# The third weave string of a two-layer decoder trunk: preparation steps placed one by one, gate columns at the end

## The chip, the cores and the metric

One core of one Trainium2 chip runs the whole program. The metric is device time in microseconds (us): the median of three runs of the kernel before is 1687.29 us, with the lowest at 1686.63 and the highest at 1689.68. The engines are named as in the profile: PE (matrix products and transposes), DVE (vector), ACT (activation), POOL (general purpose), SP (issues loads).

## The reference, cut to what matters

A trunk of two layers over 512 tokens of width 1024. In each layer five attention branches read one projection of the input; each branch's output is projected by its own matrix and scaled by a sigmoid gate of the input; the sum goes through one output matrix, and a mixture of experts follows.

```python
o_moba = merge_heads(moba_attention(heads(q, N_MOBA_HEADS), heads(k, N_MOBA_HEADS), heads(v, N_MOBA_HEADS),
                                    alibi_slopes(N_MOBA_HEADS)))
o_mla = mla_attention(c_q, c_kv, k_rope_in, g_cq, g_ckv, w_uq, w_ukv)
...
for i, o in enumerate((o_sb, o_moba, o_mla, o_nsa, o_mem)):
    gate = jax.nn.sigmoid(x @ w_gate[i] + b_gate[i])
    merged = merged + gate * (o @ w_br[i])
return merged @ w_out
```

The latent attention (`mla_attention`) first normalizes two low-rank inputs, then forms keys and values from one and queries from the other, and turns 32 columns of key and query by position (rope).

## The kernel before

All products are done three times, on values split in two parts (`hi` on ACT, L93, and the residual `lo` on DVE, L108), so nearly every product is followed by one ACT and one DVE instruction that read it from PSUM, or has such a pair ahead of it for its weights. PSUM has eight tiles of 128x512: three with the tag `f`, two `s`, two `pt`, one `pv` (L1682). Instructions run in the order of their engine's queue; the tile framework orders them by the program, and a tile with a tag waits until the readers of the tile that had its place are done.

`mixer` (L911) runs five stages in each layer. In each of them `weave` (L867) takes steps from up to three generators by a string: one letter, one step. The third stage, at about 197 to 359 us in layer 0 and 1039 to 1200 us in layer 1, has

- `a`, 20 steps, `moba_att` (L456): four heads with five steps each. For each of four query blocks `score_block` (L240) multiplies scores into an `s` tile, adds a strip and takes the minimum on DVE (L254), takes the exponent on ACT (L259) and scales on DVE (L260, L262); `to_pt` transposes into `pt`, and ACT and DVE copy that to `pth` and `ptl`. The fifth step multiplies by the values into `pv` and adds two halves (L280, L281).
- `g`, 16 steps, `gates` (L777): eight columns of the gate of the branch before (stick-breaking attention), two steps each. The first splits the weights (`wh`, from a load in `rw`; `bh`), runs 24 products into an `f` tile (L166) and takes the tanh on ACT (`gt`, L788). The second runs six products of the branch's output into another `f` tile (L116), which DVE multiplies into `gt` (L797) and POOL adds to `mg` (L798).
- `q`, 13 steps, `mla_qkv` (L469), which prepares the next stage's latent attention. In order: the input `c_kv` (with 24 products into `f`); the two parts of `c_q`; the rotary key; normalizing and weights `uw`; two steps for two pairs of heads' keys (`qk`); two steps for the values, two tiles each (step 7 writes the first two, step 8 the other two, each read by an ACT and a DVE cast into a tile with the tag `v`, of which there are six); a step that scales `c_q` (`mt` to `cp`, L534, L101, L113); and four query heads, of which each runs six products into an `f` tile and then reads it with L99 on ACT and L113, L591, L592 on DVE.

The values of MoBA (four `v` tiles) are read by the `pv` products until its last head is done, so two of the latent attention's four `v` tiles can be written only then. After the stage come preparations of the fourth branch (L625 and on) in the same `f` tiles.

Of the kernel before, what the change touches and what calls it, by code (L numbers as in the profile page):

```python
# [70 lines left out]
class Trunk:  # L71
# [1568 lines left out]
    qs = "pp"  # L1640
    wq = "ssss"
    busy_e = 3
    orders = ('aaaqaaaaqaaaaaaaaaaaaqqa', 'gggqqgaaaaggaaaaaaggaaaaqqggggggaqqqqagagaaa', 'qaagaaggagqqaggaaaqaggaqaaaaqggaqqaaaaggqggqqggqq', 'ggqgaaaaaaaaaaagqgaaaggqagggggggqqqqgaaaaga', 'ggaaaaaaaaaggggggggaaaaaaaaaaaaaaaagaaaaaaaaaagggagg')
    x1 = 0

    class _Pool:
# [66 lines left out]
```

## Time and profile before

| | us |
|---|---|
| median of three runs | 1687.29 |
| profiled execution | 1692.76 |
| its span | 1690.9 |
| PE busy in it | 1597.3 (94%) |
| DVE busy | 1248.6 (74%) |
| ACT busy | 866.4 (51%) |
| POOL busy | 258.4 (15%) |

The mean granted clock of the span is 0.977. A view of waits lists, for an engine, which line waited for which instruction; a group of lines gives the mean duration of one instruction; a table of stretches gives the busy time of each engine in a piece of the span, and the clock that TensorE was granted there.

### The profile page before, as it was taken

The numbers are of one execution on the slowest core, as the hardware profiler recorded it, in microseconds if no ns is written. First come the engines' busy times: TensorE is split into PE (matmuls) and PEld (weight loads), VectorE is DVE, ScalarE is ACT, GpSimd is POOL, SyncE is SP. The second block draws the span as 40 slices with busy tenths as digits, with TensorE's granted clock in tenths as the row PEclk, the third lists the DMA queues.
The fourth block names the chain that finished last, engine by engine and source line by source line (L and its number), as shares of the span: only waits on it lengthen the run. The fifth ranks groups of instructions, "written<-read, shape, count | busy, mean of one in ns | idle before, by whom it ended". The sixth has DMA issues, their size and how long they took to land. (4 is left out here: it accounts for less than half of the span.)

```text
span 1690.9 us, 22740 instructions
## 1 busy us (share of the span) xinstructions
PE 1597.3 (94%) x7936; PEld 1265.6 (75%) x7936; DVE 1248.6 (74%) x2557; ACT 866.4 (51%) x1655; POOL 258.4 (15%) x212
## 2 busy tenths in 40 slices
PE   8999999999999998999699999999999999999995
PEld 6877877778777786666587778777777787766673
DVE  6777558864885678998788766488657946899987
ACT  5644446343563425788436444463434733367871
POOL 0000011101112111233300000111111111113332
PEclk9999999989999998999799999999999999999998
DMA  8232222434337757998542322223332186489964
GB/s 254 66 84 79 73 70 63 113 99 126 98 91 252 248 188 254 384 376 304 194 137 57 97 72 75 74 57 95 83 93 58 49 290 220 165 308 374 380 220 156
DMA packets 254565, 273.62 MB, mean 162 GB/s; under 512 B 38667, under 2 KB 191361, under 8 KB 254433
## 3 DMA queue, kind: packets, MB, share of 16 engines
q1 hardware_dynamic: 241032, 223.98, 41.4%
q0 software_dynamic: 13312, 47.98, 8.2%
q8 instruction: 67, 1.10, 0.3%
q14 instruction: 66, 0.53, 0.1%
q10 hardware_dynamic: 88, 0.03, 0.0%
HBM read 239.18 MB, written 32.77 MB: 161 GB/s over the span
## 5 line engine op out<-in xcount | busy, mean ns | idle before, releaser
L166 PE MATMUL f<-xh,wh 128*128 128x512 f32 (+2 forms) x1920 | 630.8, 397 | 2.5 <-ACT xh L97 1.5
L166 PEld LDWEIGHTS f<-xh,wh 128*128 128x128 f32 (+1 forms) x1920 | 355.6, 188 | 77.4 <-ACT xh L97 1.7
L166 PE MATMUL f<-xl,wh 128*128 128x512 f32 (+2 forms) x960 | 381.1, 397 | 0.0
L112 DVE TENSOR_TENSOR wh<-rw,wh 128x1024 fp32r<-128x1024 f32 (+1 forms) x174 | 228.4, 1317 | 51.0 <-ACT wh L97 49.9
L798 POOL TENSOR_TENSOR mg<-mg,gt 128x512 f32<-128x512 f32 x64 | 96.8, 1512 | 984.9 <-DVE gt L797 984.9
L166 PEld LDWEIGHTS f<-xl,wh 128*128 128x128 f32 (+1 forms) x960 | 180.7, 188 | 36.6 <-DVE xl L112 0.2
L97 ACT CAST wh<-rw 128x1024 fp32r<-128x1024 f32 (+3 forms) x178 | 178.7, 1012 | 53.9 <-PE f L192 15.5
L788 ACT ACTIVATE gt<-f,bgh 128x512 f32<-128x512 f32 x80 | 55.0, 688 | 210.9 <-PE f L166 210.8
L116 PE MATMUL f<-wh,xh 128*112 128x512 f32 (+1 forms) x564 | 157.1, 404 | 5.9 <-DVE wh L112 5.8
L116 PE MATMUL f<-oh,bh 128*128 128x512 f32 x480 | 131.2, 400 | 0.2
L116 PEld LDWEIGHTS f<-wh,xh 128*112 128x112 f32 (+1 forms) x564 | 98.7, 180 | 35.9 <-DVE wh L112 7.4
L97 ACT CAST pth<-pt 128x128 fp32r<-128x128 f32 (+1 forms) x192 | 77.4, 418 | 87.3 <-PE pt L124 81.5
L797 DVE SCALAR_TENSOR_TENSOR gt<-gt,f 128x512 f32<-128x512 f32 x64 | 43.8, 684 | 105.7 <-PE f L116 101.2
L116 PE MATMUL f<-eh,xh 128*112 128x512 f32 (+1 forms) x396 | 111.0, 400 | 1.6 <-DVE eh L112 1.6
L112 DVE TENSOR_TENSOR ptl<-pt,pth 128x128 fp32r<-128x128 f32 (+1 forms) x192 | 88.8, 473 | 24.7 <-ACT pth L97 23.1
L97 ACT CAST wh<-rp 128x1024 fp32r<-128x1024 f32 x84 | 87.3, 1053 | 33.6 <-PE pt L116 14.3
L112 DVE TENSOR_TENSOR wh<-rp,wh 128x1024 fp32r<-128x1024 f32 x74 | 97.9, 1338 | 8.5 <-ACT wh L97 7.9
L116 PE MATMUL s<-qk,qk 128*128 128x256 f32 (+7 forms) x416 | 98.5, 334 | 6.0 <-DVE st L254 2.7
L116 PEld LDWEIGHTS f<-oh,bh 128*128 128x128 f32 x480 | 89.0, 190 | 19.8 <-issue 1.0
L124 PE MATMUL pt<-ident,ne 128*128 128x128 f32 x472 | 83.7, 279 | 8.6 <-DVE ne L433 3.8
L116 PEld LDWEIGHTS s<-qk,qk 128*128 128x128 f32 (+1 forms) x416 | 66.9, 192 | 27.1 <-DVE st L254 9.3
L124 PEld LDWEIGHTS pt<-ident,ne 128*128 128x128 f32 x472 | 54.7, 141 | 42.4 <-issue 17.1
(355 smaller groups left out, 2723.7 us busy)
## 6 DMA issues: line engine op xcount, KB each, us to landing
rp<-in_w_up_dram SPq DMA_DIRECT2D x96, 512.0 KB, 14.0
rw<-in_w_gate_dram SPq DMA_DIRECT2D x80, 512.0 KB, 3.9
rp<-in_w_down_dram SPq DMA_DIRECT2D x48, 512.0 KB, 14.9
rw<-in_w_in_dram SPq DMA_DIRECT2D x38, 512.0 KB, 3.9
rw<-in_w_out_dram SPq DMA_DIRECT2D x32, 512.0 KB, 6.8
yd<-xl POOLq DMA_DIRECT2D x28, 448.0 KB, 6.9
xl<-xd POOLq DMA_DIRECT2D x24, 448.0 KB, 7.6
rb<-in_w_br_dram SPq DMA_DIRECT2D x80, 128.0 KB, 3.4
```

Source lines behind the costliest of these rows:

```text
L97: return nc.scalar.copy(out, in_)
L112: return e.tensor_tensor(out, in_, hi.bitcast(F32), ALU.subtract)
L116: self.nc.tensor.matmul(out, lhsT, rhs, start=start, stop=stop)
L124: return self.nc.tensor.transpose(out, in_, self.ident[:k, :k])
L166: self.nc.tensor.matmul(o[:M, n], a[:, k, :M], b[:, k, n], start=c + k + m == 0, stop=k == KT - 1 and m == 2, skip_group_check=cut > 1)
L788: nc.scalar.activation(t, gp, AF.Tanh, bias=self.bgh[:, b * 8 + f : b * 8 + f + 1], scale=0.5)
L797: nc.vector.scalar_tensor_tensor(t, t, 1.0, bp, ALU.add, ALU.mult)
L798: i = nc.gpsimd.tensor_tensor(m, m, t, ALU.add)
```

## The change

One string of `orders` (L1643), the one of the third stage, is another; the letters are the same in number (20 `a`, 16 `g`, 13 `q`), so the instructions are the same and only their order in the queues of this stage differs, in both layers.

```diff
-    orders = ('aaaqaaaaqaaaaaaaaaaaaqqa', 'gggqqgaaaaggaaaaaaggaaaaqqggggggaqqqqagagaaa', 'qaagaaggagqqaggaaaqaggaqaaaaqggaqqaaaaggqggqqggqq', 'ggqgaaaaaaaaaaagqgaaaggqagggggggqqqqgaaaaga', 'ggaaaaaaaaaggggggggaaaaaaaaaaaaaaaagaaaaaaaaaagggagg')
+    orders = ('aaaqaaaaqaaaaaaaaaaaaqqa', 'gggqqgaaaaggaaaaaaggaaaaqqggggggaqqqqagagaaa', 'qaaqgaagqaqgaqgaaqaggaqaqaagqagaqqgaaqgagagqagggg', 'ggqgaaaaaaaaaaagqgaaaggqagggggggqqqqgaaaaga', 'ggaaaaaaaaaggggggggaaaaaaaaaaaaaaaagaaaaaaaaaagggagg')
```

Before, the string ends with gate columns between the last query heads; after, with two gate columns in a row (`gggg`), and the last `q` stands five letters from the end. The names below carry a number: `f_469` is one tile.

The first place is PE near the end of MoBA, where the value steps of the latent attention (`f` written from `uw`) stand. Before, the last three of four value tiles and what follows:

```order
L116 MATMUL f_499_2677<-uw_445_2450,cp_442_2442 128x256 x3
L116 MATMUL f_501_2684<-uw_445_2450,cp_442_2442 128x256 x3
L116 MATMUL f_503_2691<-uw_445_2450,cp_442_2442 128x256 x3
L116 MATMUL s_507_2705<-qk_290_1583,qk_202_1174 128x256
L116 MATMUL s_507_2705<-qk_291_1584,qk_202_1174 128x256
L116 MATMUL s_511_2719<-qk_290_1583,qk_202_1174 128x384
L116 MATMUL s_511_2719<-qk_291_1584,qk_202_1174 128x384
L116 MATMUL f_505_2698<-uw_445_2450,cp_442_2442 128x256 x3
L166 MATMUL f_525_2772<-xh_1_102,wh_524_2769 128x512
L166 MATMUL f_525_2772<-xl_2_103,wh_524_2769 128x512
```

After, the last two value tiles, `f_469` and `f_471`:

```order
L116 MATMUL pv_456_2485<-pth_420_2338,v_324_1853 128x128
L116 MATMUL pv_456_2485<-ptl_421_2339,v_324_1853 128x128
L116 MATMUL f_469_2527<-uw_413_2298,cp_410_2290 128x256 x3
L116 MATMUL f_471_2534<-uw_413_2298,cp_410_2290 128x256 x3
L116 MATMUL s_477_2555<-qk_288_1577,qk_201_1171 128x384
L116 MATMUL s_477_2555<-qk_289_1578,qk_201_1171 128x384
```

and, after the 24 products of `f_485`, PE goes on so:

```order
L116 MATMUL s_491_2622<-qk_288_1577,qk_201_1171 128x512
L116 MATMUL s_491_2622<-qk_289_1578,qk_201_1171 128x512
L116 MATMUL f_495_2638<-oh_382_2132,bh_482_2572 128x512 x3
L116 MATMUL f_495_2638<-oh_383_2135,bh_482_2572 128x512 x3
L116 MATMUL s_518_2748<-qk_290_1583,qk_202_1174 128x128
L116 MATMUL s_518_2748<-qk_291_1584,qk_202_1174 128x128
L116 MATMUL s_522_2761<-qk_290_1583,qk_202_1174 128x256
L116 MATMUL s_522_2761<-qk_291_1584,qk_202_1174 128x256
L116 MATMUL f_499_2666<-cp_488_2613,uw_498_2659 128x512 x2
L124 MATMUL pt_494_2631<-ident_84,ne_492_2625 128x128 x4
L116 MATMUL f_499_2666<-cp_488_2613,uw_498_2659 128x512
L116 MATMUL f_499_2666<-cp_489_2617,uw_498_2659 128x512 x3
```

Before, the last value tiles are followed by one gate column (`f_525`) and the last attention blocks. Now they stand before a gate column (`f_485` with `f_495`), two query heads (`f_499`, `f_505`), another gate column (`f_514`) and a third query head (`f_527`), since the fourth head of MoBA (`s_518` and on, up to `pv_554`) is still to come.

The second place is ACT where the last two value tiles are read. Before, the readers (`v_504`, `v_506`) stand behind the last transposes of MoBA:

```order
L97 CAST pth_493_2662<-pt_514_2728 128x3x128
L97 CAST pth_493_2662<-pt_518_2743 128x4x128
L97 CAST v_504_2695<-f_503_2691 128x4x64
L97 CAST v_506_2702<-f_505_2698 128x4x64
L280 COPY ot_520_2759<-pv_519_2750 64x512
L788 ACTIVATE gt_526_2797<-f_525_2772,bgh_60_472 128x512
L97 CAST wh_575_3028<-rw_574_3026 128x1024
```

After, `f_469` and `f_471` are read (`v_470`, `v_472`) behind the readers of `f_499`, `f_505`, `f_514` and `f_527`:

```order
L99 ACTIVATE qk_500_2673<-ot_502_2677 32x512
L99 ACTIVATE qk_506_2698<-f_505_2691 64x512
L259 ACTIVATE ne_544_2864,st_545_2865<-ne_544_2864,st_545_2865 128x512
L99 ACTIVATE qk_506_2698<-ot_508_2702 32x512
L788 ACTIVATE gt_515_2744<-f_514_2719,bgh_60_472 128x512
L97 CAST pth_516_2746<-pt_536_2818 128x3x128
L97 CAST pth_516_2746<-pt_546_2870 128x4x128
L97 CAST wh_566_2976<-rw_565_2974 128x1024
L99 ACTIVATE qk_528_2789<-f_527_2782 64x512
L97 CAST v_470_2531<-f_469_2527 128x4x64
L97 CAST v_472_2538<-f_471_2534 128x4x64
```

The readers of the last two value tiles moved behind two query heads and a gate column that were written later than these tiles.

The third place is ACT at the end of the stage, where `f_580` (L625, the fourth branch's first product, copied by L627 into `peT`) needs an `f` tile. Before, two query heads stand ahead of the column `gt_577`:

```order
L97 CAST bh_588_3119<-rb_587_3117 128x256
L97 CAST wh_590_3124<-rw_589_3122 128x1024
L99 ACTIVATE qk_560_2979<-f_559_2972 64x512
L99 ACTIVATE qk_566_3004<-f_565_2997 64x512
L99 ACTIVATE qk_560_2979<-ot_562_2983 32x512
L788 ACTIVATE gt_577_3056<-f_576_3031,bgh_60_472 128x512
L97 CAST wh_649_3380<-rw_648_3378 128x1024
L627 COPY peT_581_3074<-f_580_3071 128x32
```

After:

```order
L788 ACTIVATE gt_561_2958<-f_560_2933,bgh_60_472 128x512
L97 CAST wh_583_3079<-rw_582_3076 128x1024
L97 CAST bh_573_3023<-rb_572_3021 128x256
L788 ACTIVATE gt_568_3004<-f_567_2979,bgh_60_472 128x512
L97 CAST wh_590_3124<-rw_589_3122 128x1024
L97 CAST oh_570_3015<-oo_359_2022 128x512
L97 CAST oh_571_3018<-oo_462_2511 128x512
L97 CAST bh_588_3119<-rb_587_3117 128x256
L788 ACTIVATE gt_577_3056<-f_576_3031,bgh_60_472 128x512
```

The query heads (`qk_560`, `qk_566` before) are gone from here; gate columns alone stand ahead of `gt_577`.

## Rows read from the trace of the kernel before

**Rows 1.** Page, part 1: engine, busy us, share of the span, instructions.

```profile
PE 1597.3 (94%) x7936; PEld 1265.6 (75%) x7936; DVE 1248.6 (74%) x2557; ACT 866.4 (51%) x1655; POOL 258.4 (15%) x212
```

**Rows 2.** PE waits, 175 to 335 us: total us, times, longest us.

```profile
PE s L116 <- DVE st L254: 1.1, 2, 0.8
PE f L625 <- ACT gt L788: 1.1, 1, 1.1
PE pt L124 <- DVE ne L262: 0.8, 1, 0.8
PE f L166 <- DVE ot L592: 0.5, 1, 0.5
PE pt L124 <- DVE ne L433: 0.4, 2, 0.2
```

**Rows 3.** Stretches: length, busy us of each engine, then granted clock, DMA share, GB/s.

```profile
310.00:315.00 5.00, 3.40 (x15) 2.14 (x14) 4.80 (x8) 2.17 (x4) 0.00 (x0) 1.00 0.36 105
315.00:320.00 5.00, 4.98 (x15) 3.96 (x16) 4.50 (x5) 1.10 (x4) 2.21 (x2) 0.66 0.33 90
```

**Rows 4.** Timeline around the tail: start, us, engine, instruction, idle before and its releaser.

```profile
314.20 0.29 PE L625 MATMUL f<-ident,kt 16*128 16x16 f32 x2 [1.09 <-ACT gt L788]
...
315.02 0.54 PE L166 MATMUL f<-xh,wh 128*128 128x512 f32 x1 [0.53 <-DVE ot L592]
```

**Rows 5.** Timeline, PE inside a gate column.

```profile
211.07 0.40 PE L166 MATMUL f<-xh,wh 128*128 128x512 f32 x1
211.31 0.39 PE L166 MATMUL f<-xl,wh 128*128 128x512 f32 x1
```

**Rows 6.** Timeline, value tiles of the latent attention.

```profile
273.27 1.46 PE L116 MATMUL f<-uw,cp 128*128 128x256 f32 x9
...
282.90 0.72 ACT L97 CAST v<-f 128x256 fp32r<-128x256 f32 x2 [1.31 <-PE pv L116]
...
283.30 0.77 DVE L112 TENSOR_TENSOR v<-f,v 128x256 fp32r<-128x256 f32 x2 [0.99 <-ACT v L97]
```

**Rows 7.** Groups by line and shape, ACT, 184 to 340 us: busy, mean ns, idle before.

```profile
L97 ACT CAST wh<-rw 128x1024 fp32r<-128x1024 f32 x16 | 16.7, 1042 | 8.1 <-PE f L166 6.2 <-DMA rw<-in_w_gate_dram 1.6 <-PE f L192 0.3
L788 ACT ACTIVATE gt<-f,bgh 128x512 f32<-128x512 f32 x11 | 7.6, 689 | 15.4 <-PE f L166 15.3
...
L259 ACT ACTIVATION_READ_ACCUMULATOR ne<-ne,st 128x1 f32 x16 | 3.0, 188 | 0.0
...
L259 ACT ACTIVATE ne<-ne,st 128x512 f32<-128x512 f32 x4 | 2.9, 721 | 1.2 <-DVE st L254 1.2
...
L101 ACT ACTIVATE cp<-mt,pcol 128x512 fp32r<-128x512 f32 x3 | 2.1, 720 | 0.8 <-DVE mt L534 0.8
```

**Rows 8.** Groups by line and shape, DVE, 184 to 340 us.

```profile
L112 DVE TENSOR_TENSOR wh<-rw,wh 128x1024 fp32r<-128x1024 f32 x16 | 20.6, 1288 | 3.4 <-ACT wh L97 3.2
L797 DVE SCALAR_TENSOR_TENSOR gt<-gt,f 128x512 f32<-128x512 f32 x10 | 6.8, 684 | 5.3 <-PE f L116 5.2
L112 DVE TENSOR_TENSOR bh<-rb,bh 128x256 fp32r<-128x256 f32 x11 | 6.8, 617 | 0.0
...
L112 DVE TENSOR_TENSOR ptl<-pt,pth 128x512 fp32r<-128x512 f32 x5 | 3.4, 689 | 2.3 <-ACT pth L97 2.3
...
L112 DVE TENSOR_TENSOR v<-f,v 128x256 fp32r<-128x256 f32 x8 | 3.2, 418 | 4.1 <-ACT v L97 4.1
L260 DVE RECIPROCAL st<-st 128x1 f32<-128x1 f32 x20 | 3.1, 153 | 0.3 <-ACT ne L259 0.2
...
L592 DVE TENSOR_TENSOR ot<-f,rope 32x512 f32<-32x512 f32 x4 | 2.8, 696 | 0.1
...
L254 DVE CUSTOM_DVE_ANT_0 ne<-s,strip 128x384 f32<-128x384 f32 x4 | 2.2, 547 | 0.7 <-PE s L116 0.7
```

**Rows 9.** Stretches around another long PE wait of this kernel.

```profile
864.00:868.00 4.00, 1.84 (x11) 1.28 (x10) 4.00 (x10) 0.00 (x0) 1.46 (x1) 1.00 0.00 0
868.00:872.00 4.00, 3.94 (x22) 3.68 (x21) 4.00 (x7) 1.53 (x3) 0.00 (x0) 0.57 0.78 253
```

## Prediction

> **What bounds the kernel now.** I read the page's busy times first: PE works 94% of the span and DVE 74% [rows 1], so the time moves only where PE stops or its clock falls. The table of waits for PE in the stage lists everything that PE waited for there in layer 0, 3.9 us [rows 2]; the names and sizes in layer 1 are the same within 0.1. Of it, 1.6 stand at the end of the stage: the fourth branch's first transpose (L625) waits 1.09 for a tanh that frees an `f` tile, and the next column 0.53 more [rows 4]. Behind these two waits TensorE's granted clock is 0.66 for 5 us, a mix of its levels 1.2 and 2.4 GHz, after 1.0 (2.4 GHz) [rows 3]: 0.34 x 5 = 1.7 us lost. So the stage loses 3.9 + 1.7 = 5.6 us a layer. That is all that a better order of the stage can give back, 11 us in two layers.
>
> **What the change removes.** The tail. The query heads, with four wide DVE passes each behind one product group, no longer stand between the last gate columns; the gate column needs one such pass. The L625 product then finds a tile that was read a column earlier. Gone: 1.09 + 0.53 + 1.7 = 3.3 us a layer. I see nothing that takes its place there, since a column gives PE 30 products, 30 x 0.24 = 7.2 us [rows 5], while DVE has about 3.4 us to do for it.
>
> **What it adds: two `f` tiles held.** The two last value tiles (`f_469`, `f_471`) are written before the fourth MoBA head, but their readers need `v` places that only the last `pv` product frees. Before, such a hold is visible too: the products at 273.27, their readers at 282.90 behind an idle ACT that waited 1.31 for `pv` [rows 6]. It cost nothing, because PE had one 24-product column and attention to do, and no second `f` tile was asked for. After, six groups (`f_485`, `f_495`, `f_499`, `f_505`, `f_514`, `f_527`) pass through the one `f` tile that is left, each behind the last reader of the one before. I follow PE's list and the readers' list side by side with the durations of before. PE's pace for a 512-column product is 0.24 [rows 5]; smaller ones I take by their columns. An instruction that follows another on ACT or DVE costs about 0.07 less than its own duration (two `v` residuals take 0.77 together, one takes 0.418) [rows 6, 8]. A hand-over between engines I take as 0.15 to 0.27.
>
> - `f_499` after `f_495`: counted from the end of `f_485`, ACT runs `gt` 0.69, `wh` 1.04, two `cp` 1.44, the exponent 0.72 and its read-out 0.19 [rows 7]; DVE follows with the reciprocal 0.15, which waits for that exponent, and the gate product 0.68 [rows 8]. With hand-overs 0.4 and less 0.4 of overlap, 4.9. PE has four transposes, two scores, six products of `f_495` and four small scores to do, 0.4 + 0.5 + 1.4 + 0.4, and a wait of 0.15 for the same `gt`: 2.85. **Wait 2.1.**
> - `f_505` after `f_499`: DVE reads `f_499` last in L592, sixteenth behind the gate product: `wh` 1.29, `bh` 0.62, five 512-wide ones at 0.69 (the rows are `ptl` and L592), and nine small ones from 0.08 to 0.55 (first and last rows: reciprocal, 384-wide reduction), together 3.2 [rows 8]: 8.5, less 16 x 0.07 = 7.4. PE has 4.2 of work: six products, four transposes, four scores, one `pv` group of eight and three transposes. **Wait 3.2**, part of it ahead of `pv` and the transposes.
> - `f_514` after `f_505`: two small ones, a sum, a reduction, and the four query passes in DVE's list come to 4.8, less 0.5 of overlap plus a hand-over, 4.45; PE has 1.4 + 0.65. **Wait 2.4.**
> - `f_527` waits 0.4 for the tanh of `f_514`, its `pv` group 0.1, and `f_532` 0.95 for the first value residual, which stands behind a `wh` of 1.29 on DVE. **1.45.** With 0.3 for `f_495` and a score behind it, this stretch comes to 0.3 + 2.1 + 3.2 + 2.4 + 1.45 = **9.4**.
>
> The Trainium skill, page "Perfetto Trace Analysis", section "Identifying Performance Opportunities", says that the same gap repeating on the engine that should be saturated can mean that there is no SBUF or PSUM left for the next tile. The trace of before has no repeating gap in this stage; by the rule the trace after would have one, at `f`.
>
> **What it adds further ahead.** An earlier place has the same shape: a gate column (`f_453`) wants the tile of a key pair (`f_426`), whose last reader stands in DVE's list behind a `wh` residual, a reciprocal, two casts and two residuals. Counted from the end of the column before, tanh 0.69, `wh` 1.04 and 1.29, and 0.7 + 1.4 + 0.7 of passes no shorter than [rows 8] shows, less the overlap: 5.8, against 3.6 of PE work: 2.2. Smaller waits of transposes and `pv` for scaled scores I sum to 1.3, the stage's start to 0.7 (0.4 before), and the 0.8 at the first head's transposes stays [rows 2]: its list of instructions is the same. Together 5.0.
>
> **The sum.** After: 9.4 + 5.0 = 14.4 us a layer; before: 5.6. Per layer +8.8, in two layers +17.6. The clock: another long wait of this kernel (PE busy 1.84 of 4 us) is followed by 4 us at 0.57, which costs 1.7 [rows 9]. The stretch has three waits of that size, and while the clock is low the waits behind it shorten, since they run against ACT and DVE; I take half of one fall a layer, 1.7 in all. Total +19.3. Against the profiled execution's own 1692.76 this is 1712.1; the median of the runs lies 5.5 below that execution, 1687.29 + 19.3 = 1706.6.
>
> Bounds: below, the waits that chains of few instructions give, without the small ones: 1.9 + 2.5 + 1.85 + 0.5, with 1.0 for `f_453`, 0.4 for the start and 0.8 that stays, 9.0, so +3.4 a layer or +7: 1694. Above, 16 us a layer and three us of low clock, 2 x 13.4 = +27: 1714. Loads cost nothing: the order of the weights on SP's queue hardly changes, and they are issued long ahead; a wait for one could shrink or grow by about 1 us. POOL's sums (L798) move with their gate columns; a DVE instruction beside one can take longer, which is why `bh` has a mean of 0.62 here, and I keep that mean.
>
> **The rivals.**
>
> - *The held tiles are covered.* If the readers of `f_499`, `f_505` and `f_514` came as early as before, when they cost no wait, only the tail would count: -3.3 a layer, 1687.3 - 6.6 = 1681. It decides from the point where each of the three reader lists is shorter than PE's work beside it (2.85, 4.2 and 2.05). For it: DVE has a quarter of its time free. Against it: the lists are 4.9, 7.4 and 4.45 long by rows of before, and each would have to lose 2 us or more. By the Trainium skill, page "Perfetto Trace Analysis", section "Identifying Performance Opportunities", interleaving regimes in which another engine is the most contended may improve the time; this change interleaves DVE-heavy query heads with PE-heavy gate columns, and by that rule this case would be the right one.
> - *They cancel.* The `f` waits come to 3 us a layer in place of 9.4, and the early ones to about what was there: 1687. For it: hand-made chains add up every step; against it, the three long waits would all have to be a third of their size.
> - *The clock falls at each long wait.* Four falls a layer (with `f_453`) of 1.7, half of them hidden: 3.4 in place of 0.85, +5.1: 1712. For it: it stands behind waits of 1.6 and 2.2 [rows 3, 9]. Against it: not every wait of that size in the trace need be followed by one.
> - *The tail stays.* If L625 still waits (`gt_577` comes late all the same): +6.6, 1713. Against it: nothing that reads a query head is left there.
>
> **How the numbers follow.** My forecast has 0.70, the clock 0.10, the tail 0.04, the cancelling case 0.08 and the covered tiles 0.08. A measurement of this kernel can tell about 0.2%, 3.4 us, from no change. The forecast is slower over all of its own range, as are the clock and the tail: slower 0.84; within 0.2%: 0.08; faster 0.08. The range goes from 1692, a little below the lower bound, to 1716, above the clock case; it leaves out the two cases at or below 1687 and a little above.
>
> **What would show it.** In the waits of PE after: `f` L116 behind DVE L797 and L592 with about 2 to 3 us each, `f` L166 behind L592 with 2 or more, in both layers; no L625 wait; ACT's `v` casts behind the last `pv`. Wrong would be: no wait of PE at `f` above 1 us in the stage (then the lists are shorter than their durations say), or an L625 wait that stays. If the waits are there and the time is still lower, something behind the stage took up the slack.

## The result

The kernel after takes 1706.57 us (median of 6 runs, 1702.2 to 1716.26), the kernel before 1686.96 (6 runs, 1685.16 to 1689.68). The ratio is 1.0110, 95% interval 1.0093 to 1.0126: slower by 1.1%. The forecast was 1706.6 in a range of 1692 to 1716. The mechanism is the one forecast; two terms of the sum were not, and their errors nearly cancelled, as shown below. The profiled execution of after took 1704.7 us with a span of 1702.9, 12 us over the profiled execution of before; the medians are 19.6 apart.

The waits of PE in the stage of layer 0, in the kernel after (the view of [rows 2]: who waited for whom, total us, times, longest):

```profile
PE f L116 <- DVE ot L592: 1.9, 1, 1.9
PE f L166 <- DVE ot L592: 1.7, 1, 1.7
PE f L116 <- DVE gt L797: 1.7, 1, 1.7
PE f L166 <- DVE qk L112: 1.6, 1, 1.6
PE pt L124 <- DVE ne L262: 1.4, 4, 0.7
PE pv L116 <- DVE ptl L112: 0.6, 2, 0.4
PE f L116 <- DVE v L112: 0.5, 1, 0.5
PE pt L124 <- DVE ne L433: 0.5, 2, 0.3
```

Four long waits at `f` tiles are new (three of them behind the two held tiles, the one behind L112 ahead of them), and the L625 row is gone. Layer 1 has the same rows within 0.1 us. In the table of stretches, from the first L480 to the first L625 of a layer (length, busy us of PE, PEld, DVE, ACT, POOL, then granted clock, DMA share, GB/s), the kernel before in layer 0 reads

```profile
199.49:314.20 114.71, 111.16 (x537) 86.97 (x536) 82.32 (x185) 62.42 (x137) 14.89 (x9) 1.00 0.26 75
```

and the kernel after, in both layers,

```profile
199.81:324.77 124.96, 114.95 (x543) 89.93 (x541) 86.80 (x191) 61.56 (x136) 15.96 (x9) 0.99 0.23 64
1043.75:1170.18 126.43, 116.73 (x542) 91.59 (x540) 86.85 (x191) 61.60 (x136) 15.97 (x9) 0.96 0.23 63
```

The stage is 10.3 and 11.7 us longer. PE's idle time in it (length less PE busy) goes from 3.6 to 10.0 and 9.7. The rest, 3.8 and 5.6 us, is PE busy for longer: six score products of the next stage now stand ahead of L625 (543 products against 537), 1.3 us, and the clock is low for a while. In layer 0 of after it falls once, behind the waits at 277 and 282 us (4-us stretches of after):

```profile
278.00:282.00 4.00, 2.31 (x11) 1.38 (x9) 3.86 (x8) 2.04 (x4) 0.00 (x0) 1.00 0.00 0
282.00:286.00 4.00, 3.72 (x10) 2.94 (x11) 3.85 (x13) 0.62 (x1) 0.00 (x0) 0.58 0.00 0
```

The 0.58 costs 0.42 x 4 = 1.7 us. In layer 1, where the two waits end at 1121.4 and 1126.4, the low stretch begins behind the first of them and is longer, 5.1 us by the same sum:

```profile
1120.00:1124.00 4.00, 2.60 (x10) 2.05 (x11) 3.77 (x9) 1.48 (x5) 0.00 (x0) 0.79 0.05 8
1124.00:1128.00 4.00, 2.37 (x8) 1.81 (x8) 3.69 (x8) 1.47 (x4) 0.00 (x0) 0.50 0.02 4
1128.00:1132.00 4.00, 4.00 (x11) 3.13 (x10) 2.29 (x8) 0.11 (x1) 0.00 (x0) 0.50 0.33 89
1132.00:1136.00 4.00, 3.93 (x20) 3.00 (x20) 0.00 (x0) 0.85 (x2) 0.00 (x0) 0.93 0.14 43
```

This sum is an upper bound: PE stands idle in a part of the low time (busy 2.37 of 4 us at 0.50), and the stage of layer 1 is 1.5 us longer than that of layer 0, not 3.4.

The tail is as forecast. Where [rows 3] showed 0.66, the stretch behind L625 is at full clock, without a wait:

```profile
325.00:330.00 5.00, 5.00 (x23) 4.04 (x23) 3.27 (x3) 0.59 (x3) 2.29 (x2) 1.00 0.45 112
```

The one `f` tile that passes from hand to hand can be followed in the timeline of after (start, us, engine, instruction, idle before and its releaser):

```profile
265.38 0.69 ACT L788 ACTIVATE gt<-f,bgh 128x512 f32<-128x512 f32 x1 [2.62 <-PE f L166]
...
269.06 0.68 DVE L797 SCALAR_TENSOR_TENSOR gt<-gt,f 128x512 f32<-128x512 f32 x1
...
269.89 0.70 PE L116 MATMUL f<-cp,uw 128*128 128x512 f32 x2 [1.66 <-DVE gt L797]
...
276.62 0.70 DVE L592 TENSOR_TENSOR ot<-f,rope 32x512 f32<-32x512 f32 x1
...
277.46 1.63 PE L116 MATMUL f<-cp,uw 128*128 128x512 f32 x6 [1.95 <-DVE ot L592]
...
281.44 0.69 DVE L592 TENSOR_TENSOR ot<-f,rope 32x512 f32<-32x512 f32 x1
...
282.28 0.47 PE L166 MATMUL f<-xh,wh 128*128 128x512 f32 x1 [1.74 <-DVE ot L592]
...
293.41 0.75 DVE L112 TENSOR_TENSOR v<-f,v 128x256 fp32r<-128x256 f32 x2
...
293.88 1.66 PE L116 MATMUL f<-oh,bh 128*128 128x512 f32 x6 [0.51 <-DVE v L112]
```

Three times the last reader ends on DVE (start and duration added: 269.74, 277.32, 282.13), and 0.15 us later PE writes the next tile. The readers of the two held value tiles run at 293.41, where [rows 6] has them directly behind MoBA's last head at 283.30; MoBA's last head ends ten us later in after, and all six groups that the prediction names (`f_485` to `f_527`) are written while the two tiles are held.

### The profile page after: what moved, and what is told of

Read it like the earlier page. It is cut to its first block, busy times and chain, and to the rows that moved or that the text cites. A ratio compares the mean times of both kernels' runs of the same rounds, so it can differ in the third digit from the quotient of the medians.

```text
span 1702.9 us, 22732 instructions
## 1 busy us (share of the span) xinstructions
PE 1598.2 (94%) x7936; PEld 1267.3 (74%) x7936; DVE 1253.2 (74%) x2557; ACT 863.5 (51%) x1655; POOL 260.7 (15%) x212
## 5 line engine op out<-in xcount | busy, mean ns | idle before, releaser
L112 DVE TENSOR_TENSOR wh<-rw,wh 128x1024 fp32r<-128x1024 f32 (+2 forms) x174 | 230.8, 1330 | 48.2 <-ACT wh L97 47.1
L797 DVE SCALAR_TENSOR_TENSOR gt<-gt,f 128x512 f32<-128x512 f32 x64 | 43.8, 684 | 113.1 <-PE f L116 108.7
L116 PE MATMUL f<-eh,xh 128*112 128x512 f32 (+1 forms) x396 | 111.2, 401 | 1.6 <-DVE eh L112 1.6
L112 DVE TENSOR_TENSOR ptl<-pt,pth 128x128 fp32r<-128x128 f32 (+1 forms) x192 | 88.8, 474 | 29.9 <-ACT pth L97 28.6
L112 DVE TENSOR_TENSOR wh<-rp,wh 128x1024 fp32r<-128x1024 f32 x74 | 98.4, 1345 | 8.3 <-ACT wh L97 7.6
L116 PEld LDWEIGHTS f<-eh,xh 128*112 128x112 f32 (+1 forms) x396 | 68.2, 177 | 23.3 <-DVE eh L112 4.9
```

What stands on the lines that cost most here:

```text
L112: return e.tensor_tensor(out, in_, hi.bitcast(F32), ALU.subtract)
L116: self.nc.tensor.matmul(out, lhsT, rhs, start=start, stop=stop)
L797: nc.vector.scalar_tensor_tensor(t, t, 1.0, bp, ALU.add, ALU.mult)
```

## The experiments

Each time is a median; the ratio is to the kernel before on the same chip. Stage is the length from the first L480 to the first L625, layer 0 and layer 1.

| kernel | us | ratio, 95% interval | stage |
|---|---|---|---|
| before, again | 1689.28 | 1.0005, 0.9996 to 1.0014 | 114.8, 114.7 |
| after, again | 1707.62 | 1.0104, 1.0086 to 1.0123 | 125.8, 124.0 |
| after, free places for both tiles | 1688.78 | 1.0005, 0.9993 to 1.0018 | 115.3, 115.0 |
| before, free places for both | 1686.50 | 0.9993, 0.9981 to 1.0005 | 114.8, 114.7 |
| after, a free place for one tile | 1698.18 | 1.0071, 1.0052 to 1.0090 | 119.3, 119.1 |
| before, query heads put ahead | 1698.17 | 1.0061, 1.0038 to 1.0083 | 120.2, 119.9 |
| the same, free places for both | 1691.60 | 1.0015, 1.0003 to 1.0027 | 115.7, 115.7 |
| after, fifth gate step earlier | 1705.39 | 1.0094, 1.0073 to 1.0116 | 126.0, 124.4 |
| the same, free places for both | 1685.76 | 0.9987, 0.9970 to 1.0003 | 114.3, 114.3 |
| that once more | 1685.00 | 0.9985, 0.9968 to 1.0001 | 114.7, 114.4 |
| before with another tail | 1689.37 | 1.0007, 0.9992 to 1.0021 | 117.1, 117.1 |
| the same, free places for both | 1695.39 | 1.0046, 1.0031 to 1.0062 | 118.9, 119.7 |

The stages can't all be compared as they stand: with the hold of after (also with the fifth gate step earlier), with one free place and with the other tail, six score products of the next stage stand ahead of L625, which in before and in the two runs of after with free places for both come behind it.

**Both kernels once more.** No edit.

> The kernel before, once more, for a second trace. The profiled execution of before was 1692.8 us, 5.5 above the median of its runs, while the profiles of before and after differ by 12 us and their medians by 19.6. Theory: a profile of about 1687 has the same waits of PE in the third stage (3.9 us a layer) and differs in how often TensorE's clock falls elsewhere, 3 to 5 us less of it at 361 to 371 us (10 us at the low level in the first trace). Rival: the waits in the stage themselves vary by 2 us or more a layer from execution to execution.

> The kernel after, once more. Theory: 1706 us within 3; the four long PE waits at f tiles (1.9, 1.7, 1.7 and 1.6 us) recur in both layers with the same sizes, and the spread of the times (1702 to 1716) follows how many low-clock stretches stand behind them. Rival: the waits themselves change size between executions by more than 0.5 us.

The waits do not vary: every row of the waits of PE comes back within 0.1 us, in before and in after, in both layers. What varies is the clock. The second execution of after has the long low stretch in layer 0 (5.1 us by the same sum, between 274 and 290) and the short one in layer 1, the other way round than the first:

```profile
274.00:278.00 4.00, 1.78 (x11) 1.32 (x10) 3.85 (x11) 1.72 (x5) 0.00 (x0) 0.77 0.61 127
278.00:282.00 4.00, 3.59 (x12) 2.80 (x10) 2.90 (x7) 2.04 (x4) 0.00 (x0) 0.50 0.00 0
282.00:286.00 4.00, 2.77 (x7) 2.22 (x8) 3.85 (x10) 0.63 (x1) 0.00 (x0) 0.50 0.00 0
286.00:290.00 4.00, 4.00 (x18) 3.23 (x17) 1.12 (x5) 0.00 (x0) 0.00 (x0) 0.95 0.44 131
```

My expectation for before named the wrong place: the low stretch behind the stage in layer 0, where 10 us were at the low level, is in both executions of before. The second has none behind L625 in layer 0 and is faster for such differences by 3.3 us of span (1687.6).

**Free places for the held tiles.** The last two value tiles get places that nobody reads any more, so that their readers need not wait for MoBA's last head; the string stays.

```diff
-    def v_split(self, ps, nh=4):
+    def v_split(self, ps, nh=4, tag="v"):
...
-        v = self.sb(self.ap, [P, nh, P], "v", F32R)
+        v = self.sb(self.ap, [P, nh, P], tag, F32R)
...
-            self.lv.append(self.v_split(vp))
+            self.lv.append(self.v_split(vp, 4, ("v", "v", "mt", "krh")[t]))
```

> The string of after, but the two last value tiles get places that are free (those of the tags mt and krh) instead of the places of MoBA's values, so their readers need not wait for the last pv product. Theory (two f tiles held): the waits f behind L797, L592 (twice) and v, 5.8 us a layer, and the low clock behind them, 1.75, are gone in both layers, and the earlier ones (f behind L112 1.6, pt 1.9) stay: 1684 to 1692 us, about 15 us under after. Rival (the order itself: DVE's lists between two query heads are too long however many tiles there are): waits of the same sum move to other readers, 1700 or more.

1688.78 us, 18.8 under after, 0.05% from before. The waits of PE in its layer 0:

```profile
PE pt L124 <- DVE ne L262: 2.1, 4, 0.9
PE f L166 <- DVE qk L112: 1.6, 1, 1.6
PE s L116 <- ACT ne L259: 1.4, 1, 1.4
PE pt L124 <- DVE ne L433: 0.5, 2, 0.3
PE pv L116 <- DVE ptl L112: 0.2, 1, 0.2
```

All four rows behind L797, L592 and `v` are gone, the stage is back at 115, and the wait behind the key residual (L112, 1.6) stays, as expected. (The row behind L259 stands behind the stage and is there in before too.) The last reader of the held tiles now runs 34 us earlier than in after, where it stood at 293.41:

```profile
259.75 0.42 DVE L112 TENSOR_TENSOR krh<-f,krh 128x256 fp32r<-128x256 f32 x1
```

So the whole loss is gone with the hold of the two `f` tiles. One more thing changes in this run: once the tiles are free, the tile framework also orders PE's list anew from `f_499` on (the six 96-row score products that stand at 279.20 in after come at 326.38). No run takes places and order apart; that the hold is the cause rests on this run together with the timeline above, where each group starts 0.15 us after the last reader of the only tile left. With the string of before the same edit changes nothing:

> The same places for the last two value tiles, with the string of before. Theory: the hold costs nothing in before, so 1687 us within 0.2%, and the waits of PE in the stage stay 3.9 us a layer. Rival: free places alone are worth as much in any order, 1680 or less.

1686.50 us, ratio 0.9993 with 1 inside its interval, and the same waits as in [rows 2]. The hold is in before too but nobody needs the tiles.

**One tile held instead of two.** As above with `("v", "v", "mt", "v")`.

> The string of after; of the two last value tiles only one gets a free place (tag mt), the other still waits for MoBA's last pv product, so one f tile is held and two rotate. Theory (the cost comes from the number of f tiles that are left): f waits between none (free places for both) and 5.8 us a layer (after): 1 to 2.5 us, at f of a gate column behind L592; 1690 to 1696 us. Rival (one free tile more is enough): no f wait behind L592, L797 or v, 1687 to 1690.

In between, and 2 us above my range: 1698.18 us, stage 119. Two waits behind L592 remain, 2.8 us, over the expected 2.5; the one behind L797 and the one behind `v` are gone:

```profile
PE f L166 <- DVE ot L592: 2.8, 2, 1.9
PE f L166 <- DVE qk L112: 1.6, 1, 1.6
```

**The hold made in the kernel before.** Only the end of the string of before is changed, so that query heads stand among MoBA's last steps while the tiles are held.

```diff
-qaagaaggagqqaggaaaqaggaqaaaaqggaqqaaaaggqggqqggqq
+qaagaaggagqqaggaaaqaggaqaaaaqggaqqagqgaqqaggaqggq
```

> The string of before with one thing of after: behind the value steps, three query steps and two gate steps are put among MoBA's last four steps (q q a g q g a q q a g g a q g g q in place of q q a a a a g g q g g q q g g q q). Theory (held f tiles are enough for the cost): f waits behind L797 and L592 of 1.5 to 2 us each come up in this order too, 4 to 6 us a layer, with low clock behind some: stage of 121 to 126 us (114.7 before), 1697 to 1707 us. Rival (after is slow for its early part, or all of its parts together): no f wait above 1 us in this piece, 1685 to 1692.

1698.17 us, at the low end of the range, and the stage 120, below it. The `f` waits are of the kind named but smaller, 1.1 behind L797 and 0.6 (layer 0) or 1.2 (layer 1) behind L592, where I had 4 to 6 a layer:

```profile
PE f L116 <- DVE gt L797: 1.1, 1, 1.1
...
PE f L116 <- DVE ot L592: 0.6, 1, 0.6
```

The clock adds to them: it is 0.97 over the stage in layer 0 and 0.99 in layer 1, and PE is busy for 114.6 and 113.6 us there in place of 111.2. With free places for both tiles:

> The same string, with free places for the last two value tiles (tags mt and krh). Theory: without held tiles the waits behind L797 and L592 that came up by putting query heads ahead go again: stage of 114 to 117 us, 1684 to 1691 us. Rival: DVE's list alone holds PE up, half of the waits or more stay.

the rows behind L797 and L592 go, the clock over the stage is 1.00 and its length 115.7. The time, 1691.60, is 6.6 under the kernel with the hold and 0.6 over my range. So the order with query heads ahead costs 0.15% by itself, and 0.6% where the tiles are held.

**The earlier wait.** The fifth gate step ahead of the second pair of keys:

```diff
-qaaqgaagqaqgaqgaaqaggaqaqaagqagaqqgaaqgagagqagggg
+qaaqgaagqaqgaqgaagqagaqaqaagqagaqqgaaqgagagqagggg
```

With free places, and twice:

> As the run with free places for both tiles and the string of after, but the fifth gate step stands ahead of the second pair of keys (q g a a g q a a g in place of q g a a q a a g g, letters as many). Theory: the gate column's f tile is then one whose reader is a tanh, and the wait of 1.6 us behind the key residual (L112) goes in both layers, other waits of 2.7 us a layer stay: 1688.8 - 3.2 = 1685.6, 1683 to 1687. Rival (DVE is late there in any order): a wait of the same size comes up at the next f tile or transpose, 1687.5 to 1690.

> Once more the string of after with free places and the fifth gate step earlier, the fastest so far, against the kernel before: 1683 to 1688 us, stage of 114.3 us in both layers; whether it is faster than before by more than 0.2% is open. Rival: 1688 or more, no gain.

1685.76 and 1685.00 us. Of the wait of 1.6 behind L112 half stays, at the next `f` tile (0.8), so a part of each answer holds; the stage is 114.3 against 115. Both intervals reach just over 1 (1.0003 and 1.0001), so that this order beats the kernel before is likely and not shown. With the hold left in:

> The string of after with the fifth gate step ahead of the second pair of keys, held tiles as in after. Theory: the wait behind the key residual (L112, 1.6) and the held-tile waits have different causes and add up: 1.6 goes or halves, the waits behind L797 and L592 (twice) and v stay within 0.3 us of 1.7, 1.9, 1.7 and 0.5: 1702 to 1706 us. Rival: time won ahead of the hold is given back in it (the first f wait grows by as much), 1706 to 1708.

1705.39, and the waits of the hold are the same as in after: 1.7, 1.9, 1.6 and 0.5; the wait of 1.6 ahead of them is halved, as without the hold. So the waits of the hold do not grow by what is won ahead of them. That time is won is not shown: the stage is as long as in after again (126.0 and 124.4 against 125.8 and 124.0), with PE idle for 0.5 us less and busy for 0.7 or more longer, and the interval, 1.0073 to 1.0116, holds the ratio of after.

**The tail alone.** The string of before with another end:

```diff
-qaagaaggagqqaggaaaqaggaqaaaaqggaqqaaaaggqggqqggqq
+qaagaaggagqqaggaaaqaggaqaaaaqggaqqaaaagqgqgqqgqgg
```

> The string of before up to MoBA's last step, then another tail: gate steps and query steps in turn and two gate steps last (g q g q g q q g q g g in place of g g q g g q q g g q q). Theory: the wait of L625 (1.1), the one behind it (0.5) and the low clock behind them (1.7 where it comes) go in both layers, the rest stays: 1681 to 1685 us. Rival (the tail's waits are DVE's total load and only move to another f tile in the tail): new f waits of 1 to 2 us a layer behind L592 or L113, 1686 to 1689.

The rival holds, 0.4 us above its range: 1689.37 us, no gain. (The stage is 2.4 us longer, with the six score products ahead of L625 in it.) The L625 row is gone, and its 1.6 us with the wait behind it come back as 1.9 in other rows, of which two are waits for the scaled `c_q` that the first query head reads:

```profile
PE f L116 <- ACT cp L101: 0.6, 1, 0.6
PE f L116 <- DVE cp L113: 0.5, 1, 0.5
PE f L116 <- DVE ot L592: 0.5, 1, 0.5
...
PE f L166 <- DVE gt L797: 0.3, 1, 0.3
```

> The same string as in the run with the new tail, with free places for the last two value tiles. Theory: as that run within 0.2%, since the hold costs nothing in that order: 1681 to 1685 us. Rival (free places help any order a little): 3 us under it or more.

A miss, in the direction that neither theory had: 1695.39 us, slower. The wait for the scaled `c_q` is 2.3 in place of 0.6:

```profile
PE f L116 <- ACT cp L101: 2.3, 1, 2.3
```

The traces show where it comes from. The instructions are the same, but with the two tiles read early the framework put DVE's list in another order: a weight residual of 1.2 us that stood behind the scaling of `c_q` (L534) now stands ahead of it, after DVE has waited 2.0 for the cast on ACT. With the tail alone:

```profile
285.12 1.29 DVE L534 TENSOR_TENSOR mt<-mt,s 128x512 f32<-128x512 f32 x2
...
289.76 1.21 DVE L112 TENSOR_TENSOR wh<-rw,wh 128x1024 fp32r<-128x1024 f32 x1
```

With the free places as well:

```profile
284.67 1.23 DVE L112 TENSOR_TENSOR wh<-rw,wh 128x1024 fp32r<-128x1024 f32 x1 [2.04 <-ACT wh L97]
...
286.64 1.28 DVE L534 TENSOR_TENSOR mt<-mt,s 128x512 f32<-128x512 f32 x2
```

So a change of places alone can also reorder a list, and here that cost 6 us between the medians, of which the two stages hold 4.4.

## Why the prediction was right

**The mechanism** holds: two tiles held (free places take 18.8 us away; one place takes the ratio from 1.0104 to 1.0071), nothing lost to it in before (ratio 0.9993), and query heads put into the hold in the order of before bring its waits up there too. The rival of covered tiles falls, since the readers' lists are as long as the rows of before said, and the rival of cancelling with it. The tail did what it was said to do: no L625 wait, and no low clock behind it. That this is worth time by itself is not shown; another tail on the string of before took the same row away and gained nothing. The Trainium skill's rule on interleaving, cited with the first rival, gets no support: with free places the interleaved order is level with before (1.0005), so here interleaving alone is worth nothing that can be measured.

**The readers' lists** were sized well. From the end of `f_485` (265.12) to `f_499` (269.89) 4.8 us passed, 4.9 forecast; from `f_499` to `f_505` 7.6, forecast 7.4; from `f_505` to the next column (282.28) 4.8, forecast 4.45.

**The waits** were too long in the forecast, because PE's own work beside the lists was sized too short. I took every product by its pace, small ones by their columns. In after:

```profile
267.62 0.62 PE L116 MATMUL s<-qk,qk 128*128 128x128 f32 x4
...
279.20 1.34 PE L116 MATMUL s<-qk,qk 96*128 96x128 f32 x6
```

where I had 0.4 and 0.65. The pace was right: in before the same six 96-row products, in a full list, take 0.69 us from their start to that of the next:

```profile
327.84 0.85 PE L116 MATMUL s<-qk,qk 96*128 96x128 f32 x6
328.53 1.53 PE L116 MATMUL f<-oh,bh 128*128 128x512 f32 x6
```

What the pace leaves out is the end of a group that a wait follows, where the last product counts whole, and the short stops within it: PE is busy for 1.22 of the 1.34 us. PE had 3.1, 4.95 and 3.1 us to do in place of 2.85, 4.2 and 2.05, so the waits are 1.66, 2.6 (1.95 with 0.40 and 0.27 ahead of `pv` and a transpose) and 1.74 in place of 2.1, 3.2 and 2.4; the last group is 0.5 in place of 1.45. The early part came to 3.2 (1.6 at `f_453`, 0.7 at the first head's transposes, 0.3 at the start, 0.6 in small ones) in place of 5.0; at `f_453` the 5.8 of the forecast is the sum of its terms before the overlap that it names is taken off. In all 9.7 us a layer, where I had 14.4.

**The clock** made up for a part of it. I had 0.85 us a layer for it in after. By low share times length, the four layers in the two executions lost 1.7, 5.1, 5.1 and 1.7. But the stages with the long fall are only 1.5 and 1.8 us longer than those with the short one, so an estimate from these is 1.7 for the short fall and 3.4 for the long one, 2.5 a layer. The rival with a fall at each long wait, 3.4 a layer, was too high by that and had not the right place: there is one fall a layer, in three at the wait of `f_505` or just behind it and in one behind the wait of `f_514`, and none just behind those of `f_453` or `f_499`. Nor did before always lose the 1.7 that I charged it: in one of four layers (layer 0 of its second execution) there was no fall behind L625, and from L625 to L660 it took 19.75 us there against 21.3 in the others. So the fall cost 1.55.

**The sum**, from the first L480 to the work behind L625 (L660), from the two executions of each kernel: 289.4 us in after for both layers together and 271.3 in before, +18.1, or 9.05 a layer; the forecast was 9.65 (8.8, and 0.85 for the clock of after). PE's idle time in it goes from 4.1 to 9.8 us a layer, +5.7, where the forecast had 14.4 - 3.9 = +10.5. PE's busy time grows by 3.4, where the forecast had 0.85 - 1.7 = -0.85. The two errors, -4.8 and +4.2, nearly cancel. In the 3.4 stand the six score products that moved ahead, 1.3 and without a term in the forecast, and by the estimate the clock, 2.5 in after less 1.2 in before (three falls of 1.55 in four layers). The 0.8 us that are left I can't place in a view. Behind the stage, after gains 3.3 us in layer 0 against the first execution of before (from L660 to the experts: 295.1 in place of 298.4), for which the forecast had no term. One part is a wait of 1.5 us for an exponent (L259) in the next stage, which is in before and not in after; the rest is a shorter low stretch at the same small products there. That the median came out at 1706.57 is thus partly luck.

## What to carry to other kernels

Before preparation is moved ahead, ask not when its input is there but when its result can be stored: a product whose reader must wait for someone else's place holds a PSUM tile until then, and with two of three tiles held every other group that needs such a tile waits for the one before it to be read. That is seen in a trace as waits of the bound engine at one tile name, each behind the last reader of the tile before, and another place for the result cures it; an order that asks for few such tiles meanwhile, as that of before, never pays for it. To size such waits, add up both lists, the readers' and the bound engine's own, with durations of each shape; a group that a wait follows counts to the end of its last product, not by its pace.

## What was not expected of the hardware

With the same waits, to 0.1 us, TensorE's clock fell to 1.2 from 2.4 GHz for two different lengths, by low share times length 1.7 us in two layers of four and 5.1 in the others. The stages differ by only 1.5 and 1.8 us for it, so these falls explain at most 4 us of the spread from 1702 to 1716 us. Over the six runs the mean granted clock goes from 0.979 in the fastest to 0.971 in the slowest; where it fell in those without a profile is not known. A long wait need not bring a fall: with one free place the waits of 1.85 and 0.94 us at `f` are followed by none in the stage. And in before it falls at the small products of the fourth branch in layer 0 and not in layer 1, where the same instructions run (4-us stretches of before):

```profile
363.00:367.00 4.00, 4.00 (x18) 3.68 (x18) 0.83 (x5) 0.82 (x5) 0.00 (x0) 0.51 1.11 252
367.00:371.00 4.00, 3.63 (x12) 2.76 (x12) 2.74 (x12) 1.62 (x8) 0.00 (x0) 0.50 0.57 139
371.00:375.00 4.00, 4.00 (x14) 3.17 (x13) 2.84 (x5) 0.81 (x3) 1.87 (x2) 0.71 0.03 8
1205.00:1209.00 4.00, 2.98 (x19) 2.54 (x20) 2.71 (x14) 1.78 (x10) 0.00 (x0) 1.00 1.22 275
1209.00:1213.00 4.00, 4.00 (x19) 3.22 (x18) 3.60 (x9) 1.40 (x6) 1.29 (x1) 1.00 0.31 73
```

That is 0.49 x 4 + 0.5 x 4 + 0.29 x 4 = 5.1 us by the same sum; layer 0 has it in both executions of before, layer 1 in neither, and in the second execution of after layer 1 has it too. What decides it stays open. The Trainium skill, page "TensorE: Matmul & The Clock Gate", section "A second HAM failure mode: psum-queue depth-cycling", tells of a kernel whose PE idles briefly between groups that cycle through PSUM and whose clock then goes up and down; the falls at the `f` waits here (1.95 and 1.7 us, one fall a layer) agree with it, though not every such wait brought one; the one at 363 us has no long wait of PE directly ahead and is not covered by it.
